# Layer 0's latent stage: tile 2's square and raw up-projection weights use buffers that are idle then, and the conditioning steps begin two tiles later

## The chip, the cores and the metric

The kernel runs on one core of one Trainium2 chip. The metric is the device time of one execution in microseconds (us); lower is better. The five engines of the core are TensorE (PE: matmuls, and transposes written as matmuls against an identity), VectorE (DVE), ScalarE (ACT), GpSimd (POOL) and SyncE (SP, which here issues most DMA loads and stores). Each engine executes its own instructions in the order in which they stand; semaphores make one engine wait for another.

## The reference

The reference is a two-layer diffusion backbone over 2048 latent tokens of width 1024, preceded by 256 context tokens, all in float32. Layer 0 mixes with multi-head latent attention and a gated linear attention side by side; layer 1 is a two-dimensional neighbourhood attention. What the change touches is the beginning of layer 0. Cut to that:

```python
h = rms_norm(x, norm_g[i]) * (1 + scale) + shift        # scale, shift, gate from the conditioning c
lat = split_cols(jnp.dot(h, w_in), EVEN_SPLITS)         # 768 q latent, 256 kv latent, 32 k_rope, ...
q = jnp.dot(rms_norm(q_lat, q_norm), w_uq)              # 8 heads of 96
kv = jnp.dot(rms_norm(kv_lat, kv_norm), w_ukv)          # 8 heads of 64 (k) + 64 (v)
q, k = rms_norm(q, q_gain), rms_norm(k, k_gain)         # then rotary embedding on 32 of the 96

def modulation(cond, w, b):                              # for c and for the context's c_ctx, per layer
    m = jnp.dot(jax.nn.silu(cond), w) + b               # w: 1024 x 3072
    return jnp.split(m[..., None, :], 3, axis=-1)
```

The modulation of layer 1 and the gate of layer 0 are not needed until later in the program; their products with `ada_w` are what the conditioning steps compute.

## The kernel before

The whole kernel is one program. Every float32 product is made as three matmuls of a high and a low part (`mm3`, lines 120 to 122: high by high, high by low, low by high), so every operand is first split: a cast to the high part on ACT or DVE, then a subtraction on DVE for the low part. A framework's scheduler sets the order of the instructions on each engine from its own estimates; the order of the Python code is only its input. Tiles come from pools with a fixed number of buffers (`bufs`); the next tile of a name waits until the one that had its buffer has been read for the last time.

The touched stage is `even_latent`. It works through 18 tiles of 128 tokens (two of context, then sixteen latent) in a software pipeline, `for s in range(NT + 2)`:

- `prep(s + 1)` loads x (L347 on SP, one buffer), squares it with a sum on ACT (the elementwise result is scratch and is written to `hlo`, the low part of a ring of two tiles; the sum goes to `ssx`), takes the power -1/2 on POOL (L220, L222), scales x on DVE (L352), transposes it in eight blocks on TensorE (`px`, L355), modulates on ACT (L106, `x<-px,modB,modA`), and splits into `hhi` (L367) and `hlo` (L368). The modulated tile is also stored to memory (`H`, L369).
- `gemm(s)` multiplies by three groups of weights W0, W1, W2, each 24 matmuls of 352 columns (`gm`); `gemm(0, 1)` does the first two tiles together at s=0. ACT copies each group to `u` (one of two `gm` banks becomes free by that) and then takes four sums of squares (`sql`).
- conditioning steps: `next(ada)`, see below.
- `up(s - 1)` transposes u (`tp`, L518), splits it into `lth` (ACT) and `ltl` (DVE, L521), one buffer each, multiplies by WU (36 matmuls of 384 columns) and wkv (12 of 512), and normalises q and k (L539 to L560).
- `fin(s - 2)` transposes q and k (L573), splits into `qkhl` (L580) and stores to QT and KT (L582).

At s=17 and later the same loop begins the weights and products of the next stage (`w_rest`, `first`).

The weights are split before they are used: `split_w` loads a raw chunk (`wraw`, L403, two buffers), ACT makes the high part (`WUh<-wraw`), DVE the low part (L411 where rows are scaled, L406 otherwise). w_uq has six chunks of 128 x 768 (393 KB each).

A conditioning job is one 512-column block of `ada_w`, for two conditioning vectors. There are eight: layer 0 blocks 4 and 5 (the gate), layer 1 blocks 0 to 5. Each is two steps of the generator `ada_steps`. The first, here called the accumulation, issues eight loads of 256 KB on SP (`adaw`, L293, two buffers) and sixteen DVE multiply-adds (L296, L298). The second, the row, is two matmuls with the `pick` matrix (L303), a load of the bias (L310), an addition on DVE (L312) and, for blocks 0 to 3, four small transposes into a bank named `tp` and a copy to modB (L320) or modA (L322); blocks 4 and 5 are stored to `gates` (L327). These two lines say when a step is taken:

```python
for _ in range((s > 1) + (s in (6, 10))):
    with tc.issue_after(self.xload.ins):
```

So there is one step for each s from 2 on, two at s=6 and s=10. Accumulations fall at s = 2, 4, 6, 7, 9, 10, 12, 14, rows at s = 3, 5, 6, 8, 10, 11, 13, 15; the rows with four transposes are those at s = 6, 8, 10, 11. `issue_after` holds an instruction until another one, here the last load of x, has been issued.

## Time and profile before

| | us |
|---|---|
| median of 3 runs | 3581.59 (3581.37 to 3582.74) |
| the profiled execution | 3587.56 |
| its span (first to last instruction) | 3585.8 |
| stage `even_latent` in it | about 0 to 545 |

The mean clock that TensorE was granted in the profiled execution is 0.988 of full speed. A profile row has the start, the duration, the engine, the line of the program, the operation, the tiles written and read (buffer numbers left out), the shape, and in brackets the idle time of the engine before it with what ended it. "PE" is TensorE, "SPq" is the SP engine's own issue of DMAs. A matmul's duration includes its passage through the array; matmuls are pipelined, so the cost of one in a sequence is the distance between two starts. Work on an engine that nobody waits for costs nothing.

### The profile page before, as it was taken

The page shows a single profiled execution, that of the slowest core. Times are in us where ns is not written, and L with a number is a line of the kernel's source. Part 1 is how long each engine was busy: PE and PEld are TensorE (multiplying, and loading weights), DVE is VectorE, ACT ScalarE, POOL GpSimd, SP SyncE. Part 2 cuts the span into 40 slices and gives each one's busy share as a digit, 9 for nine tenths or more (in the row PEclk, how much of TensorE's full clock was granted, in tenths as well). Part 3 has the DMA queues.
Part 4 walks back from the last instruction along what each step waited for, and adds up shares of the span by engine and source line. Part 5 has one row for each costly group of instructions (what it writes and reads, how often), then busy time and mean ns, then how long its engine had stood idle before and what let it go on. Part 6 is the DMA issues. An engine that isn't in the chain of part 4 may idle for free.

```text
span 3585.8 us, 53487 instructions
## 1 busy us (share of the span) xinstructions
PE 3499.2 (98%) x19260; PEld 2764.4 (77%) x19260; DVE 2380.5 (66%) x5020; ACT 1404.5 (39%) x2656; POOL 1221.8 (34%) x1364
## 2 busy tenths in 40 slices
PE   8999999999999999999999999999999999999899
PEld 6888998999996666656666878888798987555577
DVE  4677766888886777788765345454688783776721
ACT  5445551101116555555553034444422223555510
POOL 1433430100101222211321233333445544777743
PEclk9999999999999999999999999999999999999999
DMA  7555563222243243334543553555744338877654
GB/s 255 147 148 167 145 177 115 87 69 84 77 115 93 71 118 84 92 89 112 163 118 129 162 169 122 144 159 165 235 151 142 129 126 221 215 208 214 188 179 147
DMA packets 386834, 513.75 MB, mean 143 GB/s; under 512 B 61229, under 2 KB 263933, under 8 KB 380666
## 3 DMA queue, kind: packets, MB, share of 16 engines
q1 hardware_dynamic: 353242, 418.68, 40.8%
q0 software_dynamic: 21952, 62.74, 5.9%
q10 hardware_dynamic: 11376, 28.91, 2.3%
q8 instruction: 153, 2.51, 0.3%
q14 instruction: 111, 0.91, 0.1%
HBM read 330.61 MB, written 179.59 MB: 142 GB/s over the span
## 4 chain that ended last, share of the span: by engine, by line
PE 86%; DVE 4%; DMA 4%; ACT 2%; issue 2%; POOL 2%; SPq 0%; POOLq 0%; DVEq 0%; ACTq 0%
PE gm L131 8%; PE gm L129 8%; PE gm L130 8%; PE av L1000 7%; PE st L1058 4%; PE mx L699 4%; PE st L1060 3%; PE st L1059 3%; PE gm L190 2%; PE gm L191 2%; PE gm L192 2%; PE o L1634 2%; PE st L1604 2%; PE st L129 2%; PE st L131 2%; PE st L130 2%
## 5 line engine op out<-in xcount | busy, mean ns | idle before, releaser
L1049 DVE TENSOR_TENSOR acc<-acc,apt 128x512 f32<-128x512 f32 x512 | 379.8, 774 | 139.8 <-ACT apt L106 137.2
L700 DVE TENSOR_REDUCE mm<-mx 128x1 f32<-128x512 f32 (+1 forms) x656 | 390.6, 629 | 82.8 <-PE mx L699 75.8
L106 ACT ACTIVATE apt<-st 128x512 f32<-128x512 f32 (+1 forms) x592 | 345.7, 594 | 237.2 <-PE st L1060 197.8
L1000 PE MATMUL av<-apt,av 128*64 128x512 f32 (+1 forms) x1184 | 270.0, 592 | 0.0
L1058 PE MATMUL st<-aq,akh 97*128 97x512 f32 x576 | 244.8, 425 | 0.3 <-ACT apt L106 0.2
L699 PE MATMUL mx<-mk,mq 96*128 96x512 f32 (+1 forms) x656 | 242.9, 372 | 0.0
L106 ACT ACTIVATE u<-gm 128x352 f32<-128x352 f32 (+1 forms) x144 | 70.5, 497 | 435.1 <-PE gm L131 212.2
L1059 PE MATMUL st<-aq,akh 96*128 96x512 f32 x576 | 228.2, 396 | 0.0
L1060 PE MATMUL st<-aq,akl 96*128 96x512 f32 x576 | 228.0, 396 | 0.0
L106 ACT ACTIVATE opt<-opt 128x930 f32<-128x930 f32 (+9 forms) x144 | 119.4, 830 | 230.0 <-POOL opt L1805 137.2
L1505 DVE CUSTOM_DVE_ANT_1 mx<-mx,mtab 128x465 f32<-128x465 f32 (+12 forms) x576 | 180.1, 342 | 28.6 <-PE mx L1499 23.0
L1000 PEld LDWEIGHTS av<-apt,av 128*64 128x64 f32 x1184 | 80.1, 136 | 152.7 <-issue 150.1
L1765 DVE TENSOR_TENSOR opt<-st,tab 128x64 f32<-128x64 f32 (+10 forms) x576 | 143.0, 315 | 74.4 <-PE st L1605 41.1
L1640 POOL TENSOR_TENSOR oacc<-oacc,opt 128x682 f32<-128x682 f32 (+9 forms) x144 | 173.9, 1228 | 32.4 <-ACT opt L106 31.2
L1058 PEld LDWEIGHTS st<-aq,akh 97*128 97x128 f32 x576 | 108.3, 188 | 70.2 <-issue 42.1
L1060 PEld LDWEIGHTS st<-aq,akl 96*128 96x128 f32 x576 | 109.5, 190 | 25.2
L699 PEld LDWEIGHTS mx<-mk,mq 96*128 96x128 f32 x656 | 123.9, 189 | 6.1
L1059 PEld LDWEIGHTS st<-aq,akh 96*128 96x128 f32 x576 | 109.9, 191 | 17.3
L106 ACT ACTIVATE x<-px,modB,modA 128x128 f32<-128x128 f32 x272 | 99.3, 468 | 58.3 <-PE px L355 48.3
L131 PE MATMUL gm<-w0h,hlo 128*128 128x512 f32 x288 | 115.1, 400 | 5.0 <-DVE hlo L380 4.9
L1604 PE MATMUL st<-q,kt 128*128 128x480 f32 (+5 forms) x256 | 98.8, 388 | 20.0 <-DVE opt L1765 15.2
L129 PE MATMUL gm<-w0h,hhi 128*128 128x512 f32 x288 | 115.8, 402 | 2.3 <-DVE hhi L367 2.3
(594 smaller groups left out, 10296.5 us busy)
## 6 DMA issues: line engine op xcount, KB each, us to landing
q<-Q SPq DMA_DIRECT2D x48, 512.0 KB
H<-x ACTq DMA_DIRECT2D x36, 512.0 KB
adaw<-ada_w SPq DMA_DIRECT2D x64, 256.0 KB
x<-H SPq DMA_DIRECT2D x32, 512.0 KB
K1t<-okt POOLq DMA_DIRECT2D x32, 512.0 KB, 6.8
kt<-K1t SPq DMA_DIRECT2D x32, 512.0 KB
mtab<-rpb_q SPq DMA_DIRECT2D x16, 899.0 KB
QT<-qkhl SPq DMA_DIRECT2D x36, 384.0 KB
```

What stands on the lines that cost most here:

```text
L106: return self.nc.scalar.activation(out, in_, func, **kw)
L129: self.nc.tensor.matmul(out, lh(k), rh(k), start=j == 0, stop=False)
L130: self.nc.tensor.matmul(out, lh(k), rl(k), start=False, stop=False)
L131: yield self.nc.tensor.matmul(out, ll(k), rh(k), start=False, stop=j == n - 1)
L699: mm = nc.tensor.matmul(ps[:, :w], q[:A_QK, (t % 6) * P : (t % 6) * P + P], k[:A_QK, k0 : k0 + w], start=True, stop=True)
L700: nc.vector.tensor_reduce(out=m[:, t, n : n + 1], in_=ps[:, :w], axis=AX.X, op=ALU.max)
L1000: nc.tensor.matmul(O[j, nb][i * 64 : i * 64 + 64, :w], V[j, kt // TT][:, kt % TT, i * 64 : i * 64 + 64], pts[i][:, :w], start=n == 0, stop ...
L1049: self.add = nc.vector.tensor_tensor(out=acc[i][:, :w], in0=a[:, :w], in1=pts[i][:, :w], op=ALU.add)
L1058: nc.tensor.matmul(ps[:, :w], kh[: A_QK + 1, i, kq], qh[: A_QK + 1, :w], start=True, stop=False)
L1059: nc.tensor.matmul(ps[:, :w], kh[:A_QK, i, kq], ql[:A_QK, :w], start=False, stop=False)
L1060: mm = nc.tensor.matmul(ps[:, :w], kl[:A_QK, i, kq], qh[:A_QK, :w], start=False, stop=True)
L1505: nc.vector.tensor_tensor_reduce(out=s, in0=s, in1=tb[:, ri : ri + rn, ci : ci + cn], scale=1.0, scalar=-3e38, op0=ALU.add, op1=ALU.max, a ...
```

## The change

The change has three parts. First, the load of x for tile 2 is written ahead of the split of w_uq (`load_x`), and its square writes its scratch result to the buffer `lth`, which nothing uses until tile 0's `up`, and no longer to the ring's `hlo`, which tile 0's gemm reads. Second, the six raw chunks of w_uq no longer share two `wraw` buffers: four go to the two buffers each of `qn` and `kn`, which are not used until tile 0's `up`, and the last two to a `wraw` of the pool `prp`. Third, the conditioning steps begin at s=4 and no longer at s=2. Accumulations are then at s = 4, 6, 7, 9, 10, 12, 14, 16 and rows at s = 5, 6, 8, 10, 11, 13, 15, 17; the rows with four transposes at s = 8, 10, 11, 13. The last two conditioning steps fall into the iterations that had none.

```diff
--- before.py
+++ after.py
@@ -336,18 +336,23 @@
 
         return [r[:, t % self.hbufs] for r in self.ring]
 
-    def prep(self, l, t, src, pp, tag):
-
-        return self.modulate(l, t, *self.transposed(t, src, pp, tag))
-
-    def transposed(self, t, src, pp, tag, xp=None):
+    def prep(self, l, t, src, pp, tag, sq=None, x=None):
+
+        return self.modulate(l, t, *self.transposed(t, src, pp, tag, sq=sq, x=x))
+
+    def load_x(self, t, src, xp=None):
+
+        x = self.tl(xp or self.prp, [P, D], "x", bufs=1)
+        self.xload = self.nc.sync.dma_start(x[:], src[t * P : t * P + P, :])
+        return x
+
+    def transposed(self, t, src, pp, tag, xp=None, sq=None, x=None):
 
         nc, sp = self.nc, self.prp
-        x = self.tl(xp or sp, [P, D], "x", bufs=1)
-        self.xload = nc.sync.dma_start(x[:], src[t * P : t * P + P, :])
+        x = x or self.load_x(t, src, xp)
         hi, lo = self.slots(t)
         ss = self.tl(sp, [P, 2], "ssx")
-        self.act(lo.rearrange("p k t -> p (k t)"), x[:], AF.Square, accum_out=ss[:, 0:1])
+        self.act((lo if sq is None else sq).rearrange("p k t -> p (k t)"), x[:], AF.Square, accum_out=ss[:, 0:1])
         self.rpow(ss[:, 1:2], ss[:, 0:1], 1.0 / D, EPS)
         nc.vector.tensor_scalar(out=x[:], in0=x[:], scalar1=ss[:, 1:2], scalar2=None, op0=ALU.mult)
         ps = [self.tl(pp, [P, 4, P], tag[0], bufs=tag[1]) for _ in range(2)]
@@ -386,7 +391,7 @@
             pass
         return d[0]
 
-    def split_steps(self, dst, key, wp, src, K, cols, tag, step, rows=None, stage=None, place=None):
+    def split_steps(self, dst, key, wp, src, K, cols, tag, step, rows=None, stage=None, place=None, raw=None):
 
 
 
@@ -399,7 +404,10 @@
             s = slice(k0, min(k0 + step, K))
             for c0 in range(0, cols, width):
                 c = slice(c0, c0 + width)
-                w = self.tl(sp, [P, s.stop - k0, width], "wraw", bufs=bufs)
+                if raw is None:
+                    w = self.tl(sp, [P, s.stop - k0, width], "wraw", bufs=bufs)
+                else:
+                    w = raw(k0)
                 self.wload = nc.sync.dma_start(w[:], src[:, s, c])
                 if rows is None:
                     self.act(hi[:, s, c], w[:])
@@ -448,7 +456,16 @@
             nc.sync.dma_start(qkg[:], self.i["qk_gain_col"])
             gr = self.tl(wp, [P, 2, 32], "grow")
             nc.sync.dma_start(gr[:], self.i["qk_gain_row"].partition_broadcast(P))
-            wuq = self.split_w(ws, self.i["w_uq"], 6, 768, "WU", 1, rows=vec[:, 0:6])
+
+            def raw(k):
+                if k > 3:
+                    return self.tl(self.prp, [P, 1, 768], "wraw", bufs=2)
+                w = self.tl(sp, [P, A_HEADS, A_QK], ("qn", "kn")[k // 2])
+                return w[:].rearrange("p h d -> p (h d)").unsqueeze(1)
+
+            with tc.issue_after(behind.ins):
+                x2 = self.load_x(2, self.i["xin"])
+                wuq = self.split_w(ws, self.i["w_uq"], 6, 768, "WU", 1, rows=vec[:, 0:6], raw=raw)
             wkv = self.split_w(wp, self.i["w_ukv"], 2, 1024, "wkv", 1, rows=vec[:, 6:8])
             ct = self.tl(wp, [P, 16, 32], "cosT")
             sn = self.tl(wp, [P, 16, 32], "sinT")
@@ -603,12 +620,13 @@
             for s in range(NT + 2):
                 if 0 < s < NT - 1:
                     with tc.issue_after(behind.ins) if s == 1 else ExitStack():
-                        hT[s + 1] = self.prep(0, s + 1, self.i["xin"], pp, px)
+                        sq = self.tl(sp, [P, 8, P], "lth", F32R, bufs=1)[:] if s == 1 else None
+                        hT[s + 1] = self.prep(0, s + 1, self.i["xin"], pp, px, sq, x2 if s == 1 else None)
                 if s == 0:
                     gemm(0, 1)
                 elif 1 < s < NT:
                     gemm(s)
-                for _ in range((s > 1) + (s in (6, 10))):
+                for _ in range((s > 3) + (s in (6, 10))):
                     with tc.issue_after(self.xload.ins):
                         next(ada, None)
                 for f, d in ((up, 1), (fin, 2)):
```

(Line numbers behind the insertions grow: the scale of x is L357, its transposes L360, hhi and hlo L372 and L373, the H store L374, the raw loads L411, the low parts of weights L419 and L414, the scale of u L507 and L508, its transposes L535, ltl L538.)

ACT where the gemm of tiles 0 and 1 ends; x_543 before and x_314 now are tile 2's x, u_384 and u_411 (u_386 and u_413 now) the results of tiles 0 and 1. Before:

```order
L106 ACTIVATE sql_518,ssl_517<-u_384 128x512
L106 ACTIVATE WUh_314<-wraw_316,lnorm_308 128x768
L106 ACTIVATE u_411<-gm_439 128x352
L106 ACTIVATE WUh_314<-wraw_320,lnorm_308 128x768
L106 ACTIVATE WUh_314<-wraw_324,lnorm_308 128x768
L106 ACTIVATE u_384<-gm_465 128x352
L106 ACTIVATE hlo_88,ssx_545<-x_543 128x1024
L106 ACTIVATE sql_518,ssl_517<-u_384 128x256
L106 ACTIVATE WUh_314<-wraw_328,lnorm_308 128x768
L106 ACTIVATE sql_518,ssl_517<-u_384 128x256
```

Now:

```order
L106 ACTIVATE sql_520,ssl_519<-u_386 128x512
L106 ACTIVATE lth_545,ssx_546<-x_314 128x1024
L106 ACTIVATE WUh_316<-qn_318,lnorm_308 128x768
L106 ACTIVATE WUh_316<-qn_322,lnorm_308 128x768
L106 ACTIVATE u_413<-gm_441 128x352
L106 ACTIVATE WUh_316<-kn_326,lnorm_308 128x768
L106 ACTIVATE WUh_316<-kn_330,lnorm_308 128x768
L106 ACTIVATE WUh_316<-wraw_334,lnorm_308 128x768
L106 ACTIVATE u_386<-gm_467 128x352
L106 ACTIVATE x_314<-px_551,modB_7_71,modA_5_69 128x128 x4
```

The square of tile 2 has moved ahead of the copies of w_uq and writes lth; the first half of tile 2's modulation now stands between the copies of the two tiles' W2 results.

TensorE at the same place, where tile 1's W2 (gm_491, gm_493 now) ends and tile 2's W0 (gm_696, gm_697 now) begins. Before:

```order
L122 MATMUL gm_491<-W2h_290,hlo_88 128x352
L355 MATMUL px_550<-ident_58,x_543 128x128 x4
L355 MATMUL px_551<-ident_58,x_543 128x128 x4
L518 MATMUL tp_575<-ident_58,u_384 128x128 x4
L518 MATMUL tp_582<-ident_58,u_384 128x128 x4
L120 MATMUL gm_696<-W0h_221,hhi_87 128x352
L121 MATMUL gm_696<-W0l_222,hhi_87 128x352
L120 MATMUL gm_723<-W1h_272,hhi_87 128x352
```

Now, the second half of tile 2's transposes, and W0 up to its second k:

```order
L121 MATMUL gm_493<-W2l_291,hhi_87 128x352
L122 MATMUL gm_493<-W2h_290,hlo_88 128x352
L360 MATMUL px_552<-ident_58,x_314 128x128 x4
L120 MATMUL gm_697<-W0h_221,hhi_87 128x352
L121 MATMUL gm_697<-W0l_222,hhi_87 128x352
L122 MATMUL gm_697<-W0h_221,hlo_88 128x352
L120 MATMUL gm_697<-W0h_221,hhi_87 128x352
L121 MATMUL gm_697<-W0l_222,hhi_87 128x352
```

The first half of the transposes (px_551) stands 24 matmuls earlier now, ahead of tile 1's W2, and the transposes of u (tp) stand 24 matmuls later, behind the first half of W0 and W1.

DVE in the iteration s=2, between tile 0's q and k and tile 1's ltl (ltl_823 before, ltl_790 now); x_666 and x_667 are tile 3, adac the accumulators. Before:

```order
L539 COPY vn_591<-up_633 128x256
L551 TENSOR_TENSOR qn_589<-qn_589,sqk_592 128x768
L539 COPY vn_591<-up_642 128x256
L368 TENSOR_TENSOR hlo_88<-x_666,hhi_87 128x512
L298 TENSOR_SCALAR adac_120_788<-adaw_810,condT_73,adac_120_788 128x512
L298 TENSOR_SCALAR adac_121_789<-adaw_810,condT_73,adac_121_789 128x512
L367 COPY hhi_87<-x_666 128x512
L555 TENSOR_REDUCE sqk_592<-sql_658 128x8
L521 TENSOR_TENSOR ltl_823<-tp_824,lth_822 128x512
L521 TENSOR_TENSOR ltl_823<-tp_831,lth_822 128x512
L298 TENSOR_SCALAR adac_120_788<-adaw_814,condT_73,adac_120_788 128x512
L298 TENSOR_SCALAR adac_121_789<-adaw_814,condT_73,adac_121_789 128x512
```

Now:

```order
L566 TENSOR_REDUCE sqk_593<-sql_653 128x8
L556 COPY vn_592<-up_634 128x256
L372 COPY hhi_87<-x_667 128x512
L568 TENSOR_TENSOR qn_590<-qn_590,sqk_593 128x768
L373 TENSOR_TENSOR hlo_88<-x_667,hhi_87 128x512
L372 COPY hhi_87<-x_667 128x512
L538 TENSOR_TENSOR ltl_790<-tp_791,lth_789 128x512
L373 TENSOR_TENSOR hlo_88<-x_667,hhi_87 128x512
L538 TENSOR_TENSOR ltl_790<-tp_798,lth_789 128x512
L556 COPY vn_592<-up_643 128x256
```

The multiply-adds are gone from here, and vn's second copy stands behind tile 1's ltl.

DVE in the iteration s=16; x_4775 before and x_4735 now are tile 17, u_4553 and u_4513 tile 16's latents, ltl_4628 and ltl_4588 tile 15's. Before:

```order
L559 TENSOR_TENSOR kn_4367<-kn_4367,sqk_4369 128x8x64
L352 TENSOR_SCALAR x_4775<-x_4775,ssx_4777 128x1024
L312 TENSOR_TENSOR adab_4623<-tp_4620,adab_4623 2x512
L491 TENSOR_SCALAR u_4553<-u_4553,ssl_4607 128x256
L490 TENSOR_SCALAR u_4553<-u_4553,ssl_4607 128x768
L521 TENSOR_TENSOR ltl_4628<-tp_4629,lth_4627 128x512
L367 COPY hhi_87<-x_4775 128x512
L521 TENSOR_TENSOR ltl_4628<-tp_4636,lth_4627 128x512
```

Now:

```order
L296 TENSOR_SCALAR adac_722_4857<-adaw_4859,condT_73 128x512
L298 TENSOR_SCALAR adac_722_4857<-adaw_4863,condT_73,adac_722_4857 128x512
L312 TENSOR_TENSOR adab_4583<-tp_4580,adab_4583 2x512
L296 TENSOR_SCALAR adac_723_4858<-adaw_4859,condT_73 128x512
L507 TENSOR_SCALAR u_4513<-u_4513,ssl_4567 128x768
L357 TENSOR_SCALAR x_4735<-x_4735,ssx_4737 128x1024
L298 TENSOR_SCALAR adac_723_4858<-adaw_4863,condT_73,adac_723_4858 128x512
L508 TENSOR_SCALAR u_4513<-u_4513,ssl_4567 128x256
L538 TENSOR_TENSOR ltl_4588<-tp_4589,lth_4587 128x512
L298 TENSOR_SCALAR adac_722_4857<-adaw_4867,condT_73,adac_722_4857 128x512
L298 TENSOR_SCALAR adac_723_4858<-adaw_4867,condT_73,adac_723_4858 128x512
L538 TENSOR_TENSOR ltl_4588<-tp_4596,lth_4587 128x512
```

Six of the sixteen multiply-adds now stand around tile 16's scale, tile 17's scale and the two ltl of tile 15; the other ten follow behind the second ltl.

## The prediction

> **What bounds the kernel now.** I read the page's first part and its chain first, then busy time by stretch, then TensorE's waits in the stretches that the change touches, and last the rows around each wait. The page:
>
> ```profile
> span 3585.8 us, 53487 instructions
> PE 3499.2 (98%) x19260; PEld 2764.4 (77%) x19260; DVE 2380.5 (66%) x5020; ACT 1404.5 (39%) x2656; POOL 1221.8 (34%) x1364
> PE 86%; DVE 4%; DMA 4%; ACT 2%; issue 2%; POOL 2%; SPq 0%; POOLq 0%; DVEq 0%; ACTq 0%
> ```
>
> TensorE is busy for 98% and carries 86% of the chain, so only its idle time and its slow clock can be won. The rows below are busy time by stretch (start:end, length, then PE, weight load, DVE, ACT, POOL, and last PE clock, DMA share, GB/s): the start of the loop up to the first conditioning row (118.82), and two pieces of it.
>
> ```profile
> 53.85:118.82 64.97, 57.35 (x322) 53.62 (x322) 42.45 (x68) 36.97 (x88) 21.70 (x38) 0.89 0.54 165
> 64.00:70.00 6.00, 4.95 (x19) 4.15 (x20) 4.48 (x7) 5.86 (x20) 3.13 (x5) 0.50 0.45 146
> 92.00:98.00 6.00, 3.65 (x11) 3.65 (x12) 6.00 (x12) 0.00 (x0) 0.86 (x2) 0.50 0.35 94
> ```
>
> The start loses 7.6 us to idle time and more to a clock of 0.89. TensorE's own rows there, and one row of its waits by group (total, times, longest) for two short ones:
>
> ```profile
> 53.85 0.43 PE L120 MATMUL gm<-W2h,hhi 128*128 128x352 f32 x1
> 61.47 0.32 PE L122 MATMUL gm<-W2h,hlo 128*128 128x352 f32 x1
> 64.67 1.97 PE L355 MATMUL px<-ident,x 128*128 128x128 f32 x8 [2.88 <-DVE x L352]
> 68.98 0.66 PE L120 MATMUL gm<-W0h,hhi 128*128 128x352 f32 x1 [0.35 <-DVE hhi L367]
> 94.35 0.69 PE L122 MATMUL up<-WUh,ltl 128*128 128x384 f32 x1 [2.65 <-DVE ltl L521]
> 101.55 0.34 PE L122 MATMUL up<-WUh,ltl 128*128 128x384 f32 x1
> 101.72 1.04 PE L573 MATMUL tp<-ident,qn 128*96 128x128 f32 x8
> 102.52 0.41 PE L120 MATMUL gm<-W2h,hhi 128*128 128x352 f32 x1
> 106.47 0.39 PE L120 MATMUL up<-wkvh,lth 128*128 128x512 f32 x1
> 109.26 1.03 PE L573 MATMUL tp<-ident,kn 128*96 128x128 f32 x8
> PE up L120 <- DVE vn L539: 1.7, 2, 1.2
> ```
>
> Two gaps, at 61.5 to 64.7 and at 88 to 94, each followed by about six microseconds at half clock. The rates at full clock come from starts: 352 columns (61.47 - 53.85) / 47 = 0.162 us, 384 columns 101.72 - 101.55 = 0.17, 512 columns (109.26 - 106.47) / 12 = 0.23, one transpose (102.52 - 101.72) / 8 = 0.10. The stretch holds, by the loops, 168 of the first (half of one gemm over two tiles, then two tiles), 72, 24 and 56: 27.2 + 12.2 + 5.6 + 5.6 = 50.6 us. So 64.97 - 50.6 = 14.4 us are lost: 2.88 + 0.35 + 1.7 + 2.65 = 7.6 in named waits, half of the busy 4.95 and 3.65 = 4.3 by the clock, 2.5 in pieces between.
>
> **Square and raw weights of tile 2.** What delays the transposes at 64.67:
>
> ```profile
> 53.88 0.63 ACT L106 ACTIVATE sql<-u 128x512 f32<-128x512 f32 x1
> 61.79 1.05 ACT L106 ACTIVATE hlo<-x 128x1024 fp32r<-128x1024 f32 x1
> 63.87 0.75 DVE L352 TENSOR_SCALAR x<-x,ssx 128x1024 f32<-128x1024 f32 x1 [1.28 <-POOL ssx L222]
> 49.83 0.42 SPq L347 DMA_DIRECT2D x<-xin  x1
> 51.96 3.38 DMA wraw<-w_uq
> ```
>
> The square at 61.79 begins only when TensorE has read hlo for the last time (61.47). In lth it waits for the load of x alone. That is issued at 49.83 and by the 3.38 us of a 393 KB load should land near 54.0; the order puts the square right behind the squares that end at 54.6. From the end of the square with its read-out (62.9) to the first transpose took 1.75, so px is ready at 54.6 + 1.05 + 0.1 + 1.75 = 57.5, and TensorE comes to it behind half of W2, at 57.7. The 2.88 go, and their slow clock (half of 4.95, 2.5). What is late next: the new order takes the second half of W2 (24 x 0.162, to 62.0), four transposes (62.4), then W0 of tile 2 at once, which needs hhi and hlo. ACT comes to the first half's modulation behind a bank's copy at 61.3; four pieces (2.54 / 7 = 0.36 each, row below) and the cast end near 63.2, the subtraction (0.69) at 63.9: 0.75 and 0.35 of waiting, and 1.1 more for the second half behind them. These 2.2 us come in four pieces, none as long as those that were followed by a slow clock.
>
> ```profile
> 66.81 2.54 ACT x L106 x7
> 69.03 0.69 DVE L368 TENSOR_TENSOR hlo<-x,hhi 128x512 fp32r<-128x512 f32 x1
> 94.82 1.40 DVE L298 SCALAR_TENSOR_TENSOR adac<-adaw,condT,adac 128x512 f32<-128x512 f32 x2
> ```
>
> The raw chunks: six loads that went through two buffers, each behind the split before it, now go out on SP back to back, and the WUh copies and WUl splits stand in a row. No TensorE wait above names them; ACT's copies sit ahead of `u<-gm`, which frees a bank, so a late chunk can hold TensorE. I price this at nothing, covered by the 4 us of W2, and take the uncovered case as a rival.
>
> **The accumulation that leaves s=2.** Eight loads and sixteen adds of 0.70 us (1.40 for two, above), 11.2 us of DVE, leave the stretch that ends at 98. Window 92 to 98 shows DVE busy 6.00 of 6.00 while TensorE waits 2.65 for ltl and 1.7 for vn. The vn and ltl waits then rest on other things. I replayed the new order with the rates above: 62.4 + 2.2 + 48 x 0.162 + 8 x 0.10 = 73.2, where 36 WU matmuls follow closed up (6.3, to 79.5), then 12 of wkv and 16 transposes (2.8 + 1.6, to 83.9). Tile 1's hi copy comes next: lth has one buffer, free only behind the last wkv, and ACT first modulates four pieces of tile 3 (1.45) and then copies (some 0.4): 1.8 idle. Its ltl stands behind a cast on DVE (0.69 and some 0.5): 1.2. Together they are near the 1.7 + 2.65 that cost a slow clock, so I add one, half of 3.65, 1.8, and 0.5 for tile 2, and 0.8 of the pieces, a third. After: 2.2 + 3.0 + 1.8 + 0.5 + 0.8 = 8.3 against 14.4, a gain of 6.1. Bounds: 14.4 if all goes; 2.6 if x is late (below).
>
> [...]
>
> **Middle.** The waits of 118.82 to 440 by group (total, times, longest), and the two slow windows:
>
> ```profile
> PE up L122 <- DVE ltl L521: 3.8, 4, 1.8
> PE tp L518 <- DVE modA L322: 1.9, 1, 1.9
> PE tp L573 <- DVE qkhl L580: 1.1, 1, 1.1
> PE px L355 <- DVE x L352: 0.7, 2, 0.4
> PE tp L518 <- DVE modB L320: 0.4, 1, 0.4
> 216.00:220.00 4.00, 2.79 (x9) 2.79 (x10) 3.73 (x7) 0.06 (x1) 0.00 (x0) 0.68 0.52 170
> 350.00:354.00 4.00, 3.89 (x15) 3.63 (x16) 4.00 (x8) 1.31 (x3) 0.00 (x0) 0.57 0.58 147
> ```
>
> Seven accumulations stand there before and after at the same s; only their jobs shift by two, and with them the rows with transposes, from s = 6, 8, 10, 11 to 8, 10, 11, 13. At s=6 and 7 the modB wait (0.4), the long ltl wait (1.8) and its clock (half of 2.79, 1.4) should go: -3.6. A transposing row comes to s=13; the dear one (modA, 1.9 and 0.43 of 3.89 = 1.7) bounds it at 3.6, nothing from below; half, 1.8, is taken. Net -1.8, between -3.6 and 0.
>
> **Tail.** One accumulation now stands at s=16 and a row at s=17.
>
> ```profile
> 440.00:466.00 26.00, 26.00 (x158) 23.35 (x157) 14.53 (x29) 13.78 (x34) 9.08 (x19) 1.00 0.33 93
> 208.74 13.05 SPq L293 DMA_DIRECT2D adaw<-ada_w  x6
> 431.57 0.35 SPq L347 DMA_DIRECT2D x<-xin  x1
> 465.78 0.34 SPq L376 DMA_DIRECT2D x<-H  x1
> DVE qkhl L580 <- ACT qkhl L106: 4.5, 2, 2.6
> DVE hhi L367 <- ACT x L106: 2.6, 2, 2.2
> DVE x L352 <- POOL ssx L222: 2.6, 1, 2.6
> ```
>
> DVE has 26.0 - 14.53 = 11.5 us free in 440 to 466, just the 11.2 wanted (the last three rows are what it waits for there). Price by the seven jobs of the middle: (7.9 idle + 3.1 clock) / 7 = 1.6. Bounds: 0 (it fits), 5.1 (the dearest, s=6 and 7, with 1.1 + 0.4 + 0.4 + 1.8 + 1.4). The loads pass SP's queue ahead of `x<-H`, the QT and KT stores and `w_rest`. Six of them took 13.05 us to issue, so eight about 17.4; behind the x load of that tile (431.57, some 6 earlier now) they are out by 449, ahead of 465.78, and I cost them at nothing. The row at s=17 is two matmuls and one DVE add, within a stretch without a PE wait.
>
> **Sum.** -6.1 - 1.8 + 1.6 = -6.3. The profiled execution took 3587.56 us (span 3585.8 and 1.8 around it), 6.0 above the median of the runs, 3581.59; the difference is taken over to the median: 3575.3. What a measurement here can tell from no change is 0.2%, 7.2 us: below 3574.4 counts as faster, above 3588.8 as slower.
>
> **Rivals.**
> The start closes almost fully and the tail is free: the replay's waits of 1.8 and 1.2 do not come since ACT and DVE run ahead, and no slow clock. 3.4 us of small waits and pieces stay, gain 11.0, and nothing in the middle or the tail: 3570.6. For it speaks the empty DVE; against it the single lth.
>
> The gain is taken back on ACT: the square now stands ahead of the copies in order. By the slowest load of x in the trace (5.47 us, below) x lands at 55.3, 1.3 later; everything behind the square, the bank's release too, slips by 1.3 and the gap brings the clock down for 2.2: 3.5 less, 3578.8.
>
> ```profile
> 200.11 5.47 DMA x<-xin
> ```
>
> No slow clock behind 1.8 and 1.2 of idle: taken singly, one is as long as the shortest gap that was followed by one (1.8), the other shorter. Then 1.8 more is won: 3573.5. [...]
>
> Slower: the accumulation at s=16 holds tile 17. Its adds stand between `u`, ltl, the x scale and hhi of that tile, each behind its load. DVE's waits there, 4.5 + 2.6 + 2.6 = 9.7 of the 11.5 free, may be unfillable, since they follow from the tile's own chain; then 11.2 - 1.8 = 9.4 come on top, and where the adds go at the pace of the loads 17.4 - 11.2 = 6.2 more: 15.6. Against -7.9 from the rest that is +7.7: 3589.3. It decides once the last load is issued behind 465.78. Against it: the middle bears the same load seven times at 1.6 each.
>
> **Chances.** Forecast 0.36 (0.13 of it below 3574.4), the closed start 0.20, the clock 0.10, taken back 0.22, slower 0.12. Faster 0.43, same 0.45, slower 0.12. The range takes the bounds: 3568 (nearly all of the 14.4 at the start), 3587 (nothing won, tail at 5.1).
>
> **What would show it.** Right: no wait for `x` L357 near 58, the first conditioning row of the program near 165, TensorE's 480th matmul of this stage some 6 us earlier than 118.82, clock above 0.95 in 53 to 112, DVE idle for loads gone there, a wait of 1 to 2 us at about 85 for lth or ltl. Wrong: a gap of over 2 us at 58 to 64, `u<-gm` waiting behind WUh, idle TensorE between 440 and 490, or `x<-H` issued behind 475.

## The result, and the profile after

| us | before | after |
|---|---|---|
| median of 10 runs each | 3581.48 | 3589.39 |
| lowest and highest | 3569.74, 3584.92 | 3578.62, 3594.08 |
| the profiled execution | 3587.56 | 3590.74 |

The changed kernel is slower by a fraction of a per cent, clear of the noise: the ratio estimated from all runs is 1.0028, with a 95% interval of 1.0017 to 1.0039, and the medians differ by +7.9 us (their quotient is 1.0022). The forecast was -6.3 us and a range of 3568 to 3587: the size and the sign both came out otherwise.

The page of the changed kernel, its first lines and its chain:

```profile
span 3588.8 us, 53484 instructions
PE 3495.2 (97%) x19260; PEld 2760.0 (77%) x19260; DVE 2382.8 (66%) x5020; ACT 1403.0 (39%) x2656; POOL 1222.2 (34%) x1364
PE 81%; DVE 7%; DMA 5%; POOL 3%; issue 2%; ACT 2%; SPq 0%; POOLq 0%; DVEq 0%; ACTq 0%
```

Five points of the chain have moved from TensorE to DVE, DMA and POOL. Busy time by stretch, changed kernel (start:end, length, PE, weight load, DVE, ACT, POOL, PE clock, DMA share, GB/s):

```profile
53.85:118.82 64.97, 60.15 (x363) 56.04 (x362) 35.36 (x54) 40.35 (x96) 20.87 (x38) 1.00 0.49 156
84.00:92.00 8.00, 5.99 (x35) 4.98 (x34) 5.93 (x12) 5.22 (x14) 2.25 (x4) 1.00 0.30 79
118.82:440.00 321.18, 310.49 (x1852) 285.34 (x1850) 231.31 (x440) 161.67 (x392) 123.99 (x225) 0.98 0.51 149
340.00:346.00 6.00, 4.96 (x17) 4.69 (x18) 5.03 (x10) 1.31 (x3) 0.00 (x0) 0.50 0.46 132
397.00:403.00 6.00, 4.34 (x17) 3.83 (x16) 5.33 (x10) 1.39 (x4) 0.00 (x0) 0.54 0.55 182
440.00:466.00 26.00, 26.00 (x155) 23.29 (x153) 19.51 (x35) 11.82 (x30) 9.82 (x17) 1.00 0.62 188
```

The start is what was forecast: 363 matmuls where 322 stood before, at clock 1.00 and no longer 0.89. The middle is not: 310.49 busy against 313.18 in the kernel before, whose row is

```profile
118.82:440.00 321.18, 313.18 (x1876) 287.39 (x1876) 233.40 (x438) 164.18 (x397) 123.13 (x226) 0.99 0.53 154
```

TensorE's own rows behind its waits, changed kernel:

```profile
58.85 0.60 PE L360 MATMUL px<-ident,x 128*128 128x128 f32 x4
60.63 0.43 PE L120 MATMUL gm<-W2h,hhi 128*128 128x352 f32 x1 [1.18 <-ACT u L106]
65.75 0.43 PE L120 MATMUL gm<-W0h,hhi 128*128 128x352 f32 x1 [0.58 <-DVE hhi L372]
88.11 0.44 PE L120 MATMUL up<-WUh,lth 128*128 128x384 f32 x1 [1.64 <-ACT lth L106]
89.09 0.44 PE L122 MATMUL up<-WUh,ltl 128*128 128x384 f32 x1 [0.37 <-DVE ltl L538]
341.04 1.11 PE L535 MATMUL tp<-ident,u 128*128 128x128 f32 x4 [3.81 <-DVE modA L322]
396.71 0.33 PE L535 MATMUL tp<-ident,u 128*128 128x128 f32 x1 [1.69 <-DVE modA L322]
400.08 0.69 PE L122 MATMUL up<-WUh,ltl 128*128 128x384 f32 x1 [1.66 <-DVE ltl L538]
539.61 0.66 PE L590 MATMUL px<-ident,kn 128*96 128x128 f32 x2 [6.62 <-POOL kn L577]
```

Between 333 and 420 the kernel before waits once, 1.9 for modA (the row below covers 118.82 to 440, where it is the only wait for modA):

```profile
PE tp L518 <- DVE modA L322: 1.9, 1, 1.9
```

The changed kernel waits 3.81 + 1.69 + 1.66 = 7.2 there, with the clock at 0.50 and 0.54 behind. What DVE does ahead of these waits, changed kernel:

```profile
338.36 2.21 DVE L298 SCALAR_TENSOR_TENSOR adac<-adaw,condT,adac 128x512 f32<-128x512 f32 x3
340.49 0.42 DVE L372 CAST hhi<-x 128x512 fp32r<-128x512 f32 x1
340.82 0.16 DVE L322 SCALAR_TENSOR_TENSOR modA<-tp,ng 128x8 f32<-128x8 f32 x1
...
397.68 1.41 DVE L298 SCALAR_TENSOR_TENSOR adac<-adaw,condT,adac 128x512 f32<-128x512 f32 x2 [1.02 <-DMA adaw<-ada_w]
399.01 0.42 DVE L372 CAST hhi<-x 128x512 fp32r<-128x512 f32 x1
399.34 0.68 DVE L538 TENSOR_TENSOR ltl<-tp,lth 128x512 fp32r<-128x512 f32 x1
```

A copy of 0.16 us that frees a `tp` bank stands behind three multiply-adds (2.21), and ltl (0.68) behind two that also wait 1.02 for their load.

To add this up I use a lag: how much later than in the kernel before TensorE has done the same amount of matmul work. It comes from the starts of all matmul rows of both traces. Each matmul is weighted by the usual distance from its start to the next in the trace of before: 0.161 us for 352 columns, 0.1755 for 384, 0.2325 for 512, 0.109 for a transpose, 0.452 for a product with `pick`. Negative is ahead.

| at (us, before) | 54 | 122 | 229 | 331 | 361 | 407 | 474 | 523 | 541 | 986 |
|---|---|---|---|---|---|---|---|---|---|---|
| after | +1.1 | -5.6 | -9.4 | -8.9 | -6.1 | +0.6 | +0.5 | +1.5 | +5.4 | +4.2 |

Where both kernels have executed exactly the same matmuls the lag needs no weights: at the transposes of kn it is 539.61 - 534.73 = +4.9. Each lag compares one execution with one. Two kernels below (the last accumulation cut, the filler behind tile 17) have the changed kernel's order on every engine up to 407; from 122 to 407 they lose 6.4 and 4.9 where it loses 6.2, so a lag repeats to within some 1.5 us. The lags that some expectations quote are by rougher weights and some 2 us lower.

A lead of 9.4 us was gone before the last accumulation, the one at s=16, was reached; another 3.9 go between 523 and 541. The span ends at +3.0. The rest of +7.9 lies in which execution was profiled: that of before was 6.1 above its median, that of after 1.4. In every kernel below the lag at 541 and the measured difference of medians agree within 6 us.

### The profile page after: what moved, and what is told of

Its sections match the earlier page's. It is cut to its first block, busy times and chain, and to the rows that moved or that the text cites. A ratio compares the mean times of both kernels' runs of the same rounds, so it can differ in the third digit from the quotient of the medians.

```text
span 3588.8 us, 53484 instructions
## 1 busy us (share of the span) xinstructions
PE 3495.2 (97%) x19260; PEld 2760.0 (77%) x19260; DVE 2382.8 (66%) x5020; ACT 1403.0 (39%) x2656; POOL 1222.2 (34%) x1364
## 4 chain that ended last, share of the span: by engine, by line
PE 81%; DVE 7%; DMA 5%; POOL 3%; issue 2%; ACT 2%; SPq 0%; POOLq 0%; DVEq 0%; ACTq 0%
PE gm L131 8%; PE gm L129 8%; PE gm L130 8%; PE av L1018 6%; PE mx L717 4%; PE st L1076 4%; PE st L1077 3%; PE st L1078 3%; PE gm L190 2%; PE gm L191 2%; PE gm L192 2%; PE o L1652 2%; PE st L1622 2%; PE st L129 2%; PE st L131 2%
```

## The experiments

Medians in us, each beside that of the kernel before on the same chip. The lags are against the same trace of before.

**The parts alone.** The buffers without the later steps (first), and the later steps without the buffers (second):

```diff
--- after.py
-                for _ in range((s > 3) + (s in (6, 10))):
+                for _ in range((s > 1) + (s in (6, 10))):
--- before.py
-                for _ in range((s > 1) + (s in (6, 10))):
+                for _ in range((s > 3) + (s in (6, 10))):
```

> The changed kernel with the conditioning steps back at their old places (first step at s=2): the first two parts of the change alone. Theory one, 'rows and end': the start was won, and the loss of the changed kernel is made later, where rows with transposes hold a bank behind the accumulation's adds (profiles: +3.0 near 341 us, +6.5 near 396) and at the last kn wait (+4.3). Then these two parts alone lose nothing later: the wait of 2.88 and its slow clock go, the waits behind the accumulation at s=2 stay: 3 to 6 us below the kernel before. Theory two, 'buffers': the new buffers set another order on ACT and SP that costs later; then it is at least 4 us above the kernel before.

> The kernel before with only the conditioning steps two tiles later. 'Rows and end': the waits behind the accumulation at s=2 go (3 to 4 us won at the start), the rows near s=11 and s=13 and the end lose about 13 us, s=6 and 7 give back 4: 4 to 9 us above the kernel before. 'Buffers': not slower than the kernel before by more than 1 us.

Buffers alone: 3587.48 against 3583.57, ratio 1.0015 (1.0004 to 1.0025). Steps alone: 3589.41, ratio 1.0020 (1.0008 to 1.0031). At 122 us the lags are +3.0 and -5.5. TensorE's waits between 53.85 and 118.82 with the buffers alone:

```profile
PE up L122 <- DVE ltl L538: 5.7, 1, 5.7
PE up L120 <- DVE vn L556: 2.5, 1, 2.5
```

The 2.88 for x has gone, and the ltl wait behind the accumulation of s=2 has grown from 2.65 to 5.7, that for vn from 1.7 to 2.5: TensorE came earlier, DVE did not. The steps alone bring the start's gain of the whole change (-5.5 against -5.6), although the wait for x is still 2.78 there, and then lose it as the whole change does (3.86 for modA at 341.65, 1.76 at 396.54; lag 0.0 at 407, +4.6 at 541). So the buffers gain nothing that these traces can tell, neither alone nor on top of the steps.

**The place of the transposing rows.** Layer 1's blocks first, the two gates last, so that the rows with transposes come early:

```diff
-            ada = self.ada_steps([(0, 4), (0, 5)] + [(1, b) for b in range(6)], sp, pp, "tp")
+            ada = self.ada_steps([(1, b) for b in range(6)] + [(0, 4), (0, 5)], sp, pp, "tp")
```

> The changed kernel with the eight conditioning jobs in another order, the six of layer 1 first and the two gates of layer 0 last, so that the rows with transposes stand at s=5, 6, 8 and 10 and none at s=11 or 13; number and places of the accumulations as in the changed kernel. 'Rows and end': the 6.5 us near s=13 go, part of the 3.0 near s=11 too; 5 to 9 us below the changed kernel, so 2 above to 2 below the kernel before. A third theory, 'the load of the late accumulation' (its adds and loads at s=16 are the cost, wherever the rows stand): within 2 us of the changed kernel.

3591.63 against 3583.57, ratio 1.0026 (1.0017 to 1.0036). TensorE's waits between 118.82 and 440:

```profile
PE up L122 <- DVE ltl L538: 3.9, 3, 2.3
PE tp L535 <- DVE modB L320: 3.4, 2, 2.6
PE tp L535 <- DVE modA L322: 1.7, 1, 1.7
```

The loss at 396 is gone (lag -3.5 at 407), and 2.64, 1.71 and 2.28 are waited for between 206 and 266 instead. What is kept at 407 is lost by 523 (lag +1.2). The waits follow the rows; the sum is not helped.

**Is it the `tp` bank?** ACT copies the row's transposes out of the bank, so that the late DVE copy no longer holds it:

```diff
+            at = self.tl(sp, [P, 8], "adat")
+            self.act(at[:], pt[:, :8])
+            pt3 = at[:].rearrange("p (j c) -> p j c", j=4)
```

> The changed kernel, but ACT copies the four small transposes of a row out of the bank at once, and DVE makes modB and modA from that copy: the bank no longer waits for DVE's turn behind the adds. 'Rows and end': TensorE's waits for modA (3.81 and 1.69) and the slow clock behind them go: 6 to 9 us below the changed kernel, near the kernel before. 'The load of the late accumulation' or 'buffers': within 2 us of the changed kernel.

3585.34 against 3583.57, ratio 1.0009 (0.9999 to 1.0020). Waits between 118.82 and 440:

```profile
PE up L122 <- DVE ltl L541: 7.8, 3, 3.4
PE tp L538 <- ACT adat L106: 0.3, 1, 0.3
```

The waits for modA fall from 5.5 to 0.3, those for ltl grow from 3.0 to 7.8, and the lag at 407 is +1.7, against +0.6 without the edit. In this stage the bank was only the first thing behind DVE's queue. The time says something else: +1.8 us, not told apart from the kernel before, where the changed kernel has +7.9, and that is what the theory of the bank had forecast. The lag at 541 is +6.6 all the same, so the trace doesn't show where the time was won, and whether the edit helps stays open.

**Fewer late steps, and a late step without its work.** Double steps at s = 6, 8, 10, 12, so that the last accumulation stands at s=14 (first); and the last block with one load and two products in place of eight and sixteen, which leaves out 7/8 of its sum (second):

```diff
-                for _ in range((s > 3) + (s in (6, 10))):
+                for _ in range((s > 3) + (s in (6, 8, 10, 12))):
--- the second
-            for k in range(KD):
+            for k in range(KD if (l, b) != (1, 5) else 1):
```

> The changed kernel with two more double steps (two steps at s=6, 8, 10 and 12, not only at 6 and 10), so that the conditioning begins at s=4 as in the changed kernel and its last accumulation stands at s=14 as in the kernel before. Theory 'last accumulation': in the changed kernel and in the runs so far TensorE led by 8 us at the start and tile 17, behind the accumulation at s=16, gave it back at the end (last WU matmul of the stage at 523 to 525 us against 519.5, then a kn wait of 6.6 to 7.2 against 3.3). Then here the last WU matmul comes at or before 518, the kn wait is at most 4, and the time is 3 to 8 us below the kernel before. Rival 'an end of its own' (the stage's end is set by something that no place of the steps moves): last WU matmul again at 523 to 525 and 2 to 8 us above the kernel before.

> The changed kernel with only the first of the eight loads and the first two of the sixteen adds of the last job, at s=16; seven eighths of the product of the last gate block are left out. The load of tile 17's x stands behind Vn's store as in the changed kernel. 'Last accumulation' by its adds and loads: the last WU matmul comes 4 to 8 us earlier than in the changed kernel and the time falls by 5 to 9 us against it. Rival 'order' (the late load of tile 17's x and not the adds): last WU matmul within 1.5 us of the changed kernel's 524.4, the time within 2 us of it.

3589.67 against 3583.38, ratio 1.0016 (1.0007 to 1.0026), and 3586.71, ratio 1.0013 (1.0004 to 1.0022). Doubling moves the loss forward (2.53 for modB at 288.33; lag -1.0 at 331, +4.5 at 474, +8.9 at 541). Without the last accumulation's work the lag goes from -0.4 at 417 to -1.1 at 523, where the changed kernel goes from +0.6 to +1.5: this work costs 1.6 us there. Yet the wait for kn is 7.02, and the lag at 541 is +3.8. So the accumulation at s=16 explains neither the middle nor the end.

**One tile later in place of two.**

```diff
-                for _ in range((s > 3) + (s in (6, 10))):
+                for _ in range((s > 2) + (s in (6, 10))):
```

> The changed kernel with the first step at s=3, one tile later than in the kernel before; the last accumulation stands at s=15. 'Last accumulation': an accumulation at s=15 leaves tile 17 a tile of time, so the last WU matmul is at 518 to 521; at the start the accumulation falls on tile 3's time and a part of the gain (some 4 of 8) is kept: 0 to 5 us below the kernel before. 'An end of its own': 2 to 8 us above it.

3585.92 against 3583.38, ratio 1.0004 (0.9995 to 1.0014): below the interval of the changed kernel, and not told apart from the kernel before. From 229 (-11.9) to 407 (-2.1) it loses 9.8, as the changed kernel does (10.0), at five waits of 1.6 to 1.9 in place of three.

**The work behind tile 17.** In the instruction order, 44 matmuls of the next tiles (`gm`) stand behind the last WU matmul of tile 17 in the kernel before, and 23 in the changed one. They are the filler under tile 17's normalisation. That matmul and the transposes of kn in the kernel before, and the same matmul in the changed one:

```profile
519.48 0.34 PE L122 MATMUL up<-WUh,ltl 128*128 128x384 f32 x1
534.73 0.53 PE L573 MATMUL px<-ident,kn 128*96 128x128 f32 x2 [3.30 <-POOL kn L560]
```

```profile
524.40 0.34 PE L122 MATMUL up<-WUh,ltl 128*128 128x384 f32 x1
```

From the one to the other it takes 15.25 us before and 539.61 - 524.40 = 15.21 now. The last WU matmul comes 4.9 later: 1.5 of that is the lag at 523, and 21 x 0.161 = 3.4 are the matmuls that now stand ahead of it. The wait for kn grows by 6.62 - 3.30 = 3.3.

The calls of `first` are ordered behind that matmul in the changed kernel, and in the kernel before as a control:

```diff
-                            first(NT - 1, s - NT + 2)
-                            first(NT - 2, s - NT + 2)
+                            with tc.issue_after(self.wulast.ins) if s > NT else ExitStack():
+                                first(NT - 1, s - NT + 2)
+                                first(NT - 2, s - NT + 2)
```

> The changed kernel, with the 48 last matmuls of the next stage's first products (`first(.., 3)`) ordered behind the last WU matmul of tile 17, where 23 of them stand now (44 in the kernel before and in the buffers-only run, 19 to 29 in every run with moved steps). Theory 'filler': the chain from tile 17's last WU matmul to the kn transposes takes 15.2 us in every run, and the kn wait is what TensorE's work behind that matmul doesn't cover. 25 more matmuls of 0.16 us: the kn wait falls from 6.6 to 2.6 to 3.5 and the time by 2 to 5 us against the changed kernel. Rival 'tile 17 is late': the WU matmuls, moved forward, wait for lth and ltl of tile 17 as long as was won; kn wait plus new waits at 450 to 540 us unchanged within 1 us, and the time within 1.5 us.

> The same ordering in the kernel before, where 44 of the 48 already stand behind: a control. Both theories: within 1.5 us of the kernel before, kn wait 2.5 to 3.5.

3589.02 against 3580.37, ratio 1.0025 (1.0014 to 1.0035), and 3580.77, ratio 1.0003 (0.9994 to 1.0013). Both have 48 matmuls there now, and in the changed kernel the last WU matmul comes at 519.24. It still waits, for another tile (TensorE, ACT and DVE):

```profile
538.62 0.42 PE L591 MATMUL tp<-ident,qn 128*96 128x128 f32 x1 [6.79 <-DVE qn L525]
536.68 0.68 ACT L106 ACTIVATE qkhl<-tp,qkg 96x512 fp32r<-96x512 f32 x1 [4.78 <-DMA QT<-qkhl]
537.40 0.75 DVE L598 SCALAR_TENSOR_TENSOR qkhl<-tp,qkg,qkhl 96x512 fp32r<-96x512 f32 x1 [3.79 <-ACT qkhl L106]
538.07 0.41 DVE L525 TENSOR_TENSOR qn<-rx,rrot 128x256 f32<-128x256 f32 x1
```

The edit also moved DVE's order: a qkhl stands ahead of qn and kn. It waits 3.79 for ACT, and ACT 4.78 for a store to QT. Without the 3.79 the wait would be 3.0 (an estimate), as in the kernels with 44 matmuls and more. So the filler came in time and another delay took its place; more filler did not buy the time back.

**All accumulations cut.** One load and two products for each of the eight blocks; 7/8 of every block's sum is left out.

```diff
-            for k in range(KD):
+            for k in range(1):
```

> The changed kernel with one load and two adds in each of the eight jobs; seven eighths of each conditioning product are left out. Theory 'adds on DVE': the waits of the middle for modA and ltl (3.8, 1.7, 1.7, 1.1, 1.0 and their slow clocks) come from adds that stand ahead of the copies on DVE; they go, TensorE reaches the tail 9 to 13 us ahead of the changed kernel. At the end the kn wait of 6 to 7 stays, since 23 matmuls still stand behind. 8 to 13 us below the changed kernel. Rival 'rows' (the transposes of the rows and their banks cost, whatever the adds): at most 3 us below it.

3568.12 against 3580.37, ratio 0.9966 (0.9954 to 0.9978). The middle:

```profile
118.82:440.00 321.18, 321.11 (x1961) 298.17 (x1961) 175.39 (x355) 168.71 (x411) 121.13 (x241) 1.00 0.39 115
```

TensorE is busy for 321.11 of 321.18 at clock 1.00; every wait there of any length was due to the accumulations (their DVE work and their loads, which this cuts together; the order is sorted anew as well). From 122 to 407 the lag goes from -6.7 to -19.1, so the accumulations cost the kernel before 12.4 us there; the changed kernel, by its own +6.2, pays 18.6 for the same seven. At the end this kernel, with 23 matmuls of filler, again waits 6.62 for kn.

**Half of the adds on GpSimd.** The accumulator of the second conditioning vector as a product and a sum on GpSimd, on top of the edit that puts filler behind tile 17:

```diff
+                    if c == 1:
+                        g = a if k == 0 else self.tl(sp, [P, 512], "adag", bufs=1)
+                        nc.gpsimd.tensor_scalar(out=g[:], in0=w[:], scalar1=self.condT[:, k, c : c + 1], scalar2=None, op0=ALU.mult)
+                        if k:
+                            nc.gpsimd.tensor_tensor(out=a[:], in0=a[:], in1=g[:], op=ALU.add)
```

> The filler order of the run before and, in addition, the second accumulator's products and sums on GpSimd (a product and a sum where DVE takes one instruction), so that DVE has eight adds for each job. 'Adds on DVE': about half of the middle's loss of some 10 us goes: 4 to 8 us below the changed kernel. Rival 'POOL': GpSimd's powers for x, u, q and k stand behind the products, so the waits for x and u grow: not below the changed kernel.

3600.11 against 3580.37, ratio 1.0057 (1.0045 to 1.0069). Two rows of POOL:

```profile
335.00 2.42 POOL L297 TENSOR_SCALAR adag<-adaw,condT 128x512 f32<-128x512 f32 x1
...
339.07 1.29 POOL L299 TENSOR_TENSOR adac<-adac,adag 128x512 f32<-128x512 f32 x1
```

What DVE does in 0.70 takes 3.7 in these two rows and 3.2 on average (1.79 and 1.37, each the mean of 56; spans on POOL are rough), among the small powers and rotations that `x`, `u` and kn wait for. DVE's own multiply-adds get longer too, 0.93 in the mean where they take 0.75 in the changed kernel. TensorE waits 4.5 for POOL's accumulator once, and ltl's waits between 118.82 and 440 are 8.4 in five, where the changed kernel has 3.0.

**Spread instead of bunched.** Each accumulation in four steps of two loads and four multiply-adds, nothing left out. The row is then no step of its own: it stands in the fourth, right behind the last multiply-adds. Three steps in every iteration from s=4 on (first), two and three in turn from s=3 on, the same in the kernel before from s=2 on, and three from s=3 on (last):

```diff
-            yield
+                if k in (1, 3, 5):
+                    yield
-                for _ in range((s > 3) + (s in (6, 10))):
+                for _ in range(3 * (s > 3)):
```

> The changed kernel with each accumulation cut into four steps of two loads and four multiply-adds (the row stays a step of its own), and three such steps in every iteration from s=4 on, so that the last one falls at s=14; nothing is left out. Theory 'bunches': what costs TensorE in the middle is that sixteen multiply-adds stand in one tile's time, ahead of modA and ltl in DVE's order; spread as twelve in nearly every tile they find free time, the waits for modA and ltl of 3.8, 1.7 and 1.7 us go, and of the 11 us that the middle loses in the changed kernel (lag from -11.5 to -1.5) at most 4 remain: 4 to 8 us below the changed kernel's 3589, thus 3581 to 3585 or less. Rival 'total': every multiply-add on DVE costs wherever it stands; the middle loses its 10 us in more and smaller waits, and the time is within 2 us of the changed kernel. If the stage's end loses 3 to 5 us again (a wait of about 6.6 for kn), that loss does not hang on an accumulation at s=15 or 16.

> As the run before (accumulations in four steps of two loads and four multiply-adds), but with two steps in an even and three in an odd iteration from s=3 on: eight to twelve multiply-adds per tile, and the steps reach into the last tiles again. Theory 'bunches': the least per tile of all versions, so the middle loses least, 0 to 4 of the 11 us, and the time is 4 to 10 us below the changed kernel's. Rival 'total': within 2 us of the changed kernel. Against the run from s=4 it tells whether the stage's end loses more when steps stand at s=15 and later (kn's wait 6.6 here and less there) or in both alike.

> The kernel before with the same cut of the accumulations, two steps in an even and three in an odd iteration from s=2 on. Theory 'bunches': the waits of the middle (ltl 1.8, modA 1.9, qkhl 1.1 with two slow windows, about 11 us in all) shrink to 4 or less, and at the start four to eight multiply-adds per tile in place of sixteen shorten the wait of 2.65 for ltl: 5 to 10 us faster than before. Rival 'total': within 2 us of the kernel before.

> The changed kernel with the same cut of the accumulations and three steps in every iteration from s=3 on. It differs from the run from s=4 by one iteration alone. Theory 'bunches': same as that run within 2 us. If it differs by more, the place decides and not the spreading, and the readings of the other three runs of this kind hold for their places only.

Against 3583.17 of before:

| | median | ratio (95%) | lag at 122 | 407 | 523 | 541 | filler matmuls |
|---|---|---|---|---|---|---|---|
| after (own base 3581.48) | 3589.39 | 1.0028 (1.0017 to 1.0039) | -5.6 | +0.6 | +1.5 | +5.4 | 23 |
| three per tile from s=4 | 3581.15 | 0.9997 (0.9987 to 1.0006) | -5.2 | +0.6 | 0.0 | -0.7 | 49 |
| two and three from s=3 | 3587.33 | 1.0016 (1.0007 to 1.0025) | -0.5 | +6.6 | +6.2 | +10.2 | 28 |
| before, two and three from s=2 | 3580.99 | 0.9996 (0.9986 to 1.0007) | -0.7 | +3.2 | +2.6 | +1.2 | 49 |
| three per tile from s=3 | 3591.24 | 1.0022 (1.0012 to 1.0031) | -2.2 | +8.4 | +7.6 | +7.5 | 47 |

The first of the four spread kernels ends where the theory of bunches put it, and not for its reason: from 122 to 407 it loses 5.8, nearly the 6.2 of the changed kernel. Of the 6.1 by which it leads the changed kernel at 541, 1.5 come from the stretch from 407 to 523 and 4.6 from the end, where it wins 0.7 and the changed kernel loses 3.9. The others lose 7.1, 3.9 and 10.6 in the middle. The place of the row has a part in this: TensorE waits for the row's `adab` 2.53 in the first and 3.95 in the last of the four. In the other two it does not wait for it for more than 0.4, and they lose all the same. Bunching is not the cause, and the theory falls. In the middle the rival holds: the multiply-adds cost wherever they stand, in all four at least 3.9 us more than in the kernel before with its bunches. How much depends on the place: one iteration's difference (three per tile from s=4 or from s=3) is worth 10 us. Neither of the two near 3581 is faster than before: both intervals hold 1.

**The wait for kn.** TensorE's row behind it with three steps per tile from s=4 (first) and with two and three from s=3 (second):

```profile
533.80 0.39 PE L591 MATMUL px<-ident,kn 128*96 128x128 f32 x2 [2.31 <-DVE kn L577]
```

```profile
544.30 0.45 PE L591 MATMUL px<-ident,kn 128*96 128x128 f32 x1 [6.67 <-POOL kn L578]
```

Over all seventeen kernels: with 19 to 29 matmuls of filler (nine kernels, the changed one among them) this wait is 6.6 to 7.2, with 44 to 49 it is 2.0 to 3.5 in seven and 6.8 in the eighth, the one above with DVE's other order. From the last WU matmul to the transposes that wait it takes 14.6 to 16.4 us in sixteen of the kernels, whatever the filler, and 19.4 in that eighth one. So the amount of filler goes with the wait and its size fits; it is not sufficient where the chain itself gets longer.

## Why the prediction was wrong, point by point

| term | forecast | change of the lag |
|---|---|---|
| start, 54 to 122 | -6.1 | -6.7 |
| middle, to 407 | -1.8 | +6.2 |
| tail, to the last WU matmuls (523) | +1.6 | +0.9 |
| behind them (523 to 541) | not priced | +3.9 |
| next stage, to 986 | not priced | -1.2 |

**Start: right in size, not in its parts.** No wait for x near 58 (the transposes at 58.85 have none), the first conditioning row at 165.93, clock 1.00, and the lth wait of 1.64 at 88.11 where 1.8 was worked out. The ltl wait of 1.2 was 0.37, and no slow clock followed: that rival (the clock stays up) held here. What stands below on equal gaps (1.64 and clock 1.00 here, 1.65 and 0.72 in one of the spread kernels) shows that the length of a gap alone does not decide here, so the 1.8 were won by luck. Against them stands a term that was put at nothing, the raw chunks:

```profile
58.38 1.84 ACT L106 ACTIVATE WUh<-qn,lnorm 128x768 fp32r<-128x768 f32 x2 [1.68 <-DMA qn<-w_uq]
60.13 0.45 ACT L106 ACTIVATE u<-gm 128x352 f32<-128x352 f32 x1
```

ACT waits 1.68 for the first raw chunk, its copy of `u` stands behind two WUh copies, and TensorE waits 1.18 for that copy at 60.63. This is one of the signs of being wrong that the prediction names, in small. The share of the parts was wrong as well. The buffers were credited with 2.88 and its slow clock by themselves; alone they gain nothing, since ltl's wait takes up what x's gives back as long as the accumulation of s=2 stands there, and on top of the steps they gain nothing either.

**Middle: this is the step that failed.** "Seven accumulations stand there before and after at the same s; only their jobs shift by two", and a transposing row at s=13 bounded at 3.6 by the dearest seen. The gain at s=6 and 7 came (forecast -3.6, lag -5.6 to -9.4). But the same accumulations with other rows between them cost more: +2.8 from 331 to 361 and +6.7 from 361 to 407, where the row at s=13 meets the accumulation of s=14 and DVE holds first modA, then ltl, each with a slow clock behind (0.62 from 396.71 to 400.08, 0.50 from there to 403). By an estimate from the rows and windows above, the wait at 341 and its clock cost 6.3 (3.81 and half of 4.96), those at 396 to 400 cost 5.3 (1.69, 1.66 and 0.46 of 4.34): each is above the bound of 3.6. The bound was taken from a single row of the kernel before, as if the price of a row were its own. The cuts show that the price belongs to the accumulations; freeing the bank, other jobs, other iterations and spreading show that it moves from one wait to the next. What TensorE waits for follows DVE's order, and this differs in each kernel. Why the changed kernel's order is worse by just 6.2 than that of before stays open: no run shows it apart from a re-sorting of the whole queue.

**Tail: right in size and in its cover.** The tail took 0.9, and the accumulation's work in it 1.6, the forecast figure, by the run that leaves it out. TensorE was busy for 26.00 of 26.00 from 440 to 466, DVE rose from 14.53 to 19.51, `x<-H` was issued at 461.18, before 475. That the accumulation at s=16 holds tile 17 did not happen. The slower rival, 3589.3, has almost the measured time, by luck and not by its mechanism.

**Left out: the end of the stage.** The prediction followed the moved steps and not what the scheduler did with the next tiles' matmuls: 21 fewer of them cover tile 17's normalisation, and TensorE waits 6.62 for kn in place of 3.30. The order of the changed kernel showed this count before any run; the prediction follows it only to s=16. That the count is the cause is argued from its size, from the equal 15.2 us of the chain and from sixteen of seventeen kernels; no run changes the filler and nothing else.

## What to carry to other kernels

When work moves out of a stretch, look for the queue that it joins: sixteen multiply-adds that nobody waits for still stand in order ahead of a 0.16 us copy that TensorE does wait for, and in the trace freeing that copy only exposes the next one. Price a moved step by removing such work altogether (here 12.4 us for the seven in the middle of the kernel before, 18.6 in the changed one) and never by the dearest single wait. Where a scheduler writes the order, a move of one iteration was worth 10 us here, so compare the whole order up to the next stage, above all what covers a tile's last chain; and check that a version which meets its number does so by its mechanism.

## What was not expected of the hardware

Gaps of the same length were followed by a slow clock in some of the kernels and not in others. The wait for lth behind tile 1's transposes, 1.64 to 1.66 us long and ending between 85.9 and 88.9, stands in twelve of the kernels. In six the mean clock from 0.5 us before its end to 6 us behind it is 1.00, in the other six 0.74. Examples are the changed kernel's 1.64 (clock 1.00 in 84 to 92, above), and two of the spread kernels, three per tile from s=4 (row and window),

```profile
86.98 0.45 PE L120 MATMUL up<-WUh,lth 128*128 128x384 f32 x1 [1.65 <-ACT lth L106]
```

```profile
86.00:92.00 6.00, 4.66 (x17) 4.29 (x18) 4.26 (x9) 2.33 (x6) 1.52 (x2) 0.72 0.43 129
```

and two and three from s=3:

```profile
88.89 0.45 PE L120 MATMUL up<-WUh,lth 128*128 128x384 f32 x1 [1.66 <-ACT lth L106]
```

```profile
88.00:94.00 6.00, 4.52 (x27) 4.08 (x28) 4.41 (x9) 3.25 (x8) 1.38 (x2) 1.00 0.51 145
```

The price of a wait of this size was thus, by an estimate from these two windows, uncertain by about 1.7 us ((1.00 - 0.72) x 6), however well the wait itself was forecast.

On GpSimd a product of a 128 x 512 tile with a scalar took 1.79 us (mean of 56; 2.42 in the row above), against 0.50 for the same product on DVE in the same run (mean of 8; 0.48 in the changed kernel), and the sum of two tiles 1.37 (mean of 56), against 0.68 for a two-tile operation on DVE (ltl in the changed kernel, mean of 34). That is 3.6 times as long for the product and 2.0 times for the sum. On GpSimd the product, which reads one tile, took longer than the sum of two; on DVE it took less than the two-tile operation.
